# RWKV-7 recurrence of a streaming trunk: one elementwise step emitted later, one epilogue step earlier, filler matmuls moved

## The chip, the cores and the metric

One of the cores of a Trainium2 chip runs the whole program. The metric is device time in microseconds for one execution; lower is better. Every number below comes from the kernel before the change: its three timed runs, and one further execution that the hardware profiler recorded.

## The reference, cut to what matters

The program is one inference step of a small trunk over 1024 prompt rows and 8 x 16 sample rows (1152 in all), in float32. The part that the change touches is RWKV-7 time mixing; what is computed there:

```python
u = pr + (shifted - pr) * mu                       # token shift on the projected columns
r, k, v, wl, al, gl = split(u)
decay = exp(-exp(-softplus(-(w0 + tanh(wl) @ w2)) - 0.5))
a  = sigmoid(a0 + al @ a2);  g = sigmoid(gl) @ g2
kk = normalise(k * k_k);     k = k * (1 + (a - 1) * k_a)      # "key's part"
S_t = S_{t-1} * w_t + (S_{t-1} @ -kk_t) (kk_t a_t)^T + v_t k_t^T ;  y_t = S_t r_t
y  = groupnorm(y) * lnx_g + lnx_b
out = (y + sum(r * k * r_k) * v) * g
```

After it come forgetting attention, a gated merge and a SwiGLU block; these are not touched.

## The kernel before

The recurrence runs in chunks of 64 rows. Six units (`rwkv_unit`, called for unit 0 to 5) take 192 rows each: three chunks for all 8 heads, that is 12 blocks of two heads. Unit 5 is the last; it holds one prompt chunk and the sample rows, and has no next unit.

Inside a unit each chunk's delta rule becomes a triangular system. First the elementwise factors `BK` (L550 to L552) and `TT` (L559, L561) are made; then the Gram products (matmuls, masks L589); then a triangular inverse: VectorE inverts 16 x 16 diagonal blocks with thirty small operations (L623, L625) and turns the result twice (L637, L639); TensorE joins blocks in five steps: L661, copy `p0`; L669 and L672, followed by six VectorE additions into `x1c` and `x3`; L690, copied as `p1`; L699, copied into `x3`. Then the chunks follow one after the other: L736, L743, `w_sb`, L726, a copy into `SV4`, L748, `st`, L759, two additions, and the next chunk's L736.

TensorE's order is written out by hand: matmuls stand in its queue as the code emits them. Between the steps of the recurrence, `W(us)` emits filler: the k-steps ("pieces") of the input projection of later columns, `ceil(us / 0.52)` of them. One piece is three matmuls of 128x384 (L151, L152, L153: a float32 product in three parts), about 0.52 us by the constant `PIECE` in the code. The amount of filler over the whole program is fixed; what isn't placed here is run later. Outside of TensorE a scheduler sets each engine's order; operations inside `hi(...)` are preferred. Every queue then runs in order, and an instruction that waits holds up what stands behind it. ScalarE's queue also issues DMAs (stores of `g_s`, `oa_s`, `out_v_p`, `v_s`).

Two generators are stepped through from inside a unit:

- `prologue` of the next unit (`nxt`), seven steps: (1) `kr` L435 and its square L437; (2, 3) the two halves of the decay and iclr products L445, L446 with sigmoids L449, L450; (4) the norm's sums L454, logarithm L455, exponential L456; (5) the scan L463 and the exponentials L473 to L481; (6) **key's part**: L493 (x4), L494, L496, L500 (x4), all on VectorE; (7) the bonus L505, L506.
- `epilogue` of the unit before (`last`), three steps: (1) mean L514, L515, square L516, emitted behind the Gram products; (2) **variance**: matmuls L520, logarithm L521, exponential L522, then L523, L526, L527 on VectorE; (3) gate L532, L533 and the store `oa_s`.

Large tiles come from one ring, `tt_()`, of 13 slots: a new tile waits until all readers of the tile that had the slot are done. The small PSUM tiles come from rings too: `xs` for the products of the two generators (so L446 waits until a sigmoid, a logarithm or L533 has read an earlier one), `ms` for the rest.

Of the kernel before, what the change touches and what calls it, by code (L numbers as in the profile page):

```python
# [53 lines left out]
def hybrid_kernel(ctx: ExitStack, tc: tile.TileContext, d, o):  # L54
# [189 lines left out]
    def D(n):  # L244
        for _ in range(n):
            if fq:
                fq.pop(0)()
# [106 lines left out]
    def ms():  # L354
        return psr.tile([P, 512], F32, tag="ms", name="ms")
# [36 lines left out]
    def hi(f, *args, **kw):  # L392

        with tc.high_priority(offset=AHEAD):
            return f(*args, **kw)

    def W(us):

        D(int(math.ceil(us / PIECE)))
# [136 lines left out]
    def rwkv_unit(u_, us, nu, pre, last):  # L536
# [6 lines left out]
        nxt_pre, nxt, nus = {}, [], None  # L543

        def step(g):
            for x in g:
                next(x, None)
# [6 lines left out]
        def both(hd, i):  # L554
            return BK[HS[hd], i, 1 - hd:3 - hd, :].rearrange("p x t -> p (x t)")
# [25 lines left out]
        def masked(dst, src, c0, hs):  # L581
            n0 = 0
            late_ = [final and (c0 + n) % NC3 >= 1 for n in range(4)]
            while n0 < 4:
                n1 = n0 + 1
                while n1 < 4 and late_[n1] == late_[n0]:
                    n1 += 1
                mk = (gmask_s if late_[n0] else gmask)[hs].unsqueeze(1).broadcast_to([hs.stop - hs.start, n1 - n0, 2, C])
                V.tensor_tensor(dst[:, n0:n1], src[hs, n0:n1], mk, op=mult)  # L589
                n0 = n1  # L590

        for c0 in range(0, NC12, 4):
            pg = [(psr.tile([P, 512], F32, tag=f"y{x}", name="gram", bufs=1) if c0 == 4 else ms())
                  .rearrange("p (c y t) -> p c y t", c=4, y=2) for x in range(2)]
            for c in range(4):
                for hd in range(2):
                    T.matmul(pg[hd][:, c], both(hd, c0 + c), TT[HS[hd], c0 + c, hd], start=True, stop=True)
            for hd in range(2):
                masked(GB[HS[hd], c0:c0 + 4], pg[hd], c0, HS[hd])
                masked(TT[OP[hd], c0:c0 + 4, hd], pg[hd], c0, OP[hd])  # L600
            W(2.1)
        step(last)
        gab, grb = GB[:, :, 0, :], GB[:, :, 1, :]

# [32 lines left out]
        V.transpose(X1[:, 0:32, :], X[:, 0:32, :].rearrange("p t j -> p j t"))  # L637
        XL = inv_tile()
        V.transpose(XL[:, 0:32, :], X[:, 0:32, :])  # L639
        step(nxt)  # L640
        W(1.5)
        step(last)
        W(1.5)
        step(nxt)
        W(1.5)
        step(nxt)
        W(1.5)
        step(last)
# [1 line left out]
        step(nxt)  # L650
        W(1.5)
        step(nxt)
        W(3.1)
        xd = XL[:, 0:32, 0:NC12].rearrange("p t c -> p c t")
        QS = [slice(32 * q, 32 * q + 32) for q in range(4)]
        NB32 = NC12 * 32
# [23 lines left out]
        for q, qs in enumerate(QS):  # L680
            t0 = 32 * (q % 2)
            hi(V.tensor_tensor, x3[qs, :, t0:t0 + 32], p4[qs], xd[qs], op=add)
            if q % 2:
                hi(GP.memset, x3[qs, :, 0:32], 0.0)
        step(nxt)
        W(2.6)
        ps = ms()
        for c in range(NC12):
# [3 lines left out]
        p1 = tt_()[:, 0:NC12 * 32]  # L692
        for h0 in (0, 64):
            hi(S.copy, p1[h0 + 32:h0 + 64, :], ps[h0 + 32:h0 + 64, :NC12 * 32])
        W(1.5)
        ps = ms()
        for c in range(NC12):
            for h0 in (0, 64):
# [271 lines left out]
    with tc.manual_schedule(engines={mybir.EngineType.PE}):  # L970
        us, pre = unit_load(0), {}
        for _ in prologue(0, us, pre):
            W(5.0)
        W(2.0)
        last = []
        for u_ in range(NUN):
            us, pre, ep = rwkv_unit(u_, us, u_ + 1 if u_ + 1 < NUN else None, pre, last)
            last = [ep]
        for _ in last[0]:
            W(4.0)  # L980
# [52 lines left out]
    def head_load(h):  # L1033
        hs = slice(h * 64, (h + 1) * 64)
        need(*((kind, h // 2, g) for kind in "qkv" for g in range(NG)))
        flush()
        ka = fx.tile([P, SEQ], F32R, tag="ka", name=f"ka{h}", bufs=2)
        qa = fx.tile([P, SEQ], F32R, tag="qa", name=f"qa{h}", bufs=2)
        kb = fx.tile([68, SEQ], F32R, tag="kb", name=f"kb{h}", bufs=2)
        qb = fx.tile([68, SEQ], F32R, tag="qb", name=f"qb{h}", bufs=2)  # L1040
        vv = fx.tile([P, 8, 2, 64], F32R, tag="vv", name=f"vv{h}", bufs=2)
        for dst, srcs in ((ka, (kh_s[hs, :], kh_s[hs, :])), (qa, (qh_s[hs, :], ql_s[hs, :])),
                          (kb, (kl_s[hs, :], ka_s[h])), (qb, (qh_s[hs, :], qa_s[h]))):
            for x, s_ in enumerate(srcs):
                dma(dst[64 * x:64 * x + s_.shape[0], :].bitcast(F32), s_)
        for x in range(2):
            dma(vv[:, :, x, :].bitcast(F32), v2_s[:, x, hs].rearrange("(i p) e -> p i e", p=P))
        return ka, kb, qa, qb, vv
# [139 lines left out]
    nxt = head_load(0)  # L1188
    for h in range(8):
        hd = nxt  # L1190
        for g in range(2):
            pts = [prompt_scores(4 * g + j, *hd[:4]) for j in range(4)]
            prompt_pv(h, g, pts, *hd[4:], ())
            if g == 0 and h < 7:
                with tc.issue_after(turns[-2].ins) if h else ExitStack():
                    nxt = head_load(h + 1)
# [450 lines left out]
    with tc.tile_pool(name="fd", bufs=1, reuse_waits="tile", side="left") as fd, \  # L1647
# [7 lines left out]
        def down_ops(f):  # L1655
            raw = fd.tile([P, DM], F32, tag="wraw", name="raw_d", bufs=2)
            dma(raw, d["w_down"][0, f * P:(f + 1) * P, :])
            ar = fd.tile([P, NT], F32, tag="araw", name="raw_act", bufs=2)
            dma(ar, a_s[f * P:(f + 1) * P, :])
            wh = fd.tile([P, DM], F32R, tag="wh", name="hi_d", bufs=nbw)  # L1660
            wl = fd.tile([P, DM], F32R, tag="wl", name="lo_d", bufs=nbw)
            ah = fd.tile([P, NT], F32R, tag="ah", name="ah", bufs=nbw)
            al = fd.tile([P, NT], F32R, tag="al", name="al", bufs=nbw)
            split((wh, wl), raw)
            split((ah, al), ar)
            return wh, wl, ah, al
# [63 lines left out]
        for x in range(len(groups)):  # L1730
            nxt = [down_ops(f) for f in groups[x + 1]] if x + 1 < len(groups) else None
# [33 lines left out]
```

## Time and profile before

| | us |
|---|---|
| median of 3 runs (lowest, highest) | 2108.36 (2106.34, 2108.38) |
| the profiled execution: its own time | 2110.43 |
| the profiled execution: span on the core | 2108.4 |
| TensorE busy | 1980.6 (94% of the span) |
| VectorE busy | 1276.6 (61%) |
| ScalarE busy | 808.4 (38%) |
| mean granted TensorE clock | 0.969 of full speed |

The six units of the recurrence stand between about 190 and 800 us of the span. TensorE is busy or nearly so everywhere else. The page's slices show where it isn't: a digit under 9 in the row PE, a digit under 9 in the row PEclk. The rows that carry the argument are in their own section below. In a timeline a row gives the start, the duration, the engine, the line, the operation and the tiles, and in brackets how long the engine sat idle before it and what it waited for.

### The profile page before, as it was taken

The page shows a single profiled execution, that of the slowest core. Times are in us where ns is not written, and L with a number is a line of the kernel's source. Part 1 is how long each engine was busy: PE and PEld are TensorE (multiplying, and loading weights), DVE is VectorE, ACT ScalarE, POOL GpSimd, SP SyncE. Part 2 cuts the span into 40 slices and gives each one's busy share as a digit, 9 for nine tenths or more (in the row PEclk, how much of TensorE's full clock was granted, in tenths as well). Part 3 has the DMA queues.
Part 4 walks back from the last instruction along what each step waited for, and adds up shares of the span by engine and source line. Part 5 has one row for each costly group of instructions (what it writes and reads, how often), then busy time and mean ns, then how long its engine had stood idle before and what let it go on. Part 6 is the DMA issues. An engine that isn't in the chain of part 4 may idle for free. (4 is left out here: it accounts for less than half of the span.)

```text
span 2108.4 us, 38216 instructions
## 1 busy us (share of the span) xinstructions
PE 1980.6 (94%) x15472; PEld 1796.7 (85%) x15472; DVE 1276.6 (61%) x2414; ACT 808.4 (38%) x1567; POOL 187.1 (9%) x298
## 2 busy tenths in 40 slices
PE   7999988998899989789989899999999999799998
PEld 6999877787788978578867898999999999688887
DVE  5222777666766745578846528966666666454445
ACT  5322434362534432467744335523322323221113
POOL 1001000000000000010034236000000000000004
PEclk9999999999999999799999999999999999899999
DMA  4333333222221223677558544222222321542212
GB/s 158 105 101 98 108 92 97 70 66 67 66 70 53 80 80 95 155 202 201 138 180 258 173 146 150 73 74 63 83 63 69 99 63 53 207 149 85 85 64 90
DMA packets 221540, 228.41 MB, mean 108 GB/s; under 512 B 41534, under 2 KB 195796, under 8 KB 221364
## 3 DMA queue, kind: packets, MB, share of 16 engines
q1 hardware_dynamic: 158916, 159.33, 25.8%
q10 hardware_dynamic: 61920, 64.54, 9.1%
q8 instruction: 122, 2.00, 0.4%
q0 software_dynamic: 528, 2.10, 0.3%
q14 instruction: 54, 0.44, 0.1%
HBM read 157.00 MB, written 68.98 MB: 107 GB/s over the span
## 5 line engine op out<-in xcount | busy, mean ns | idle before, releaser
L151 PE MATMUL gm<-hh,hi_c 128*128 128x384 f32 (+1 forms) x1032 | 373.5, 362 | 2.5 <-DVE lg L916 0.7
L152 PE MATMUL gm<-hl,hi_c 128*128 128x384 f32 (+1 forms) x1032 | 351.3, 340 | 1.0 <-DVE hl L135 1.0
L153 PE MATMUL gm<-hh,lo_c 128*128 128x384 f32 (+1 forms) x1032 | 350.9, 340 | 0.0
L151 PEld LDWEIGHTS gm<-hh,hi_c 128*128 128x128 f32 (+1 forms) x1032 | 195.2, 189 | 19.7 <-issue 3.3
L152 PEld LDWEIGHTS gm<-hl,hi_c 128*128 128x128 f32 (+1 forms) x1032 | 195.7, 190 | 5.8 <-DVE hl L135 1.2
L153 PEld LDWEIGHTS gm<-hh,lo_c 128*128 128x128 f32 (+1 forms) x1032 | 195.2, 189 | 2.1
L1676 PE MATMUL dn<-hi_d,ah 128*128 128x512 f32 x396 | 156.2, 394 | 12.8 <-ACT ah L1383 12.1
L1677 PE MATMUL dn<-lo_d,ah 128*128 128x512 f32 x396 | 155.3, 393 | 0.0
L1678 PE MATMUL dn<-hi_d,al 128*128 128x512 f32 x396 | 155.3, 393 | 0.0
L1680 DVE TENSOR_TENSOR x<-x,dn 128x512 f32<-128x512 f32 x108 | 73.9, 686 | 118.3 <-PE dn L1678 116.7
L1676 PEld LDWEIGHTS dn<-hi_d,ah 128*128 128x128 f32 x396 | 75.2, 190 | 30.2 <-ACT ah L1383 13.4
L146 DVE TENSOR_TENSOR lo_c<-raw_c,hi_c 128x1024 fp32r<-128x1024 f32 (+1 forms) x43 | 51.5, 1199 | 70.2 <-ACT hi_c L145 70.1
L1696 POOL TENSOR_TENSOR yo<-x,gF 128x512 f32<-128x512 f32 x17 | 21.9, 1289 | 761.7 <-DVE x L1680 752.0
L1678 PEld LDWEIGHTS dn<-hi_d,al 128*128 128x128 f32 x396 | 75.1, 190 | 16.4 <-DVE al L1384 0.9
L1677 PEld LDWEIGHTS dn<-lo_d,ah 128*128 128x128 f32 x396 | 75.3, 190 | 15.5
L1383 ACT CAST ah<-raw_act 128x1152 fp32r<-128x1152 f32 x22 | 25.5, 1161 | 161.5 <-PE dn L1677 141.0
L1481 PE MATMUL po<-hi_o,mh 128*128 128x256 f32 x288 | 82.4, 286 | 0.0
L1482 PE MATMUL po<-lo_o,mh 128*128 128x256 f32 x288 | 82.3, 286 | 0.0
L1483 PE MATMUL po<-hi_o,ml 128*128 128x256 f32 x288 | 82.0, 285 | 0.0
L145 ACT CAST hi_c<-raw_c 128x1024 fp32r<-128x1024 f32 (+1 forms) x43 | 44.3, 1030 | 86.9 <-PE gm L152 81.9
L1564 DVE TENSOR_TENSOR buf<-buf,m 128x256 f32<-128x256 f32 (+1 forms) x88 | 39.7, 452 | 45.7 <-PE m L1542 45.7
L265 DVE SCALAR_TENSOR_TENSOR su<-gm,omu,sh 128x384 f32<-128x384 f32 (+1 forms) x42 | 24.0, 571 | 64.2 <-ACT sh L261 40.1
(500 smaller groups left out, 5354.9 us busy)
## 6 DMA issues: line engine op xcount, KB each, us to landing
raw_c<-in_w_in SPq DMA_DIRECT2D x42, 512.0 KB
raw_act<-a_s SPq DMA_DIRECT2D x22, 576.0 KB
raw_w_gate<-in_w_gate SPq DMA_DIRECT2D x22, 512.0 KB
raw_w_up<-in_w_up SPq DMA_DIRECT2D x22, 512.0 KB
raw_d<-in_w_down SPq DMA_DIRECT2D x22, 512.0 KB
g_s<-sg ACTq DMA_DIRECT2D x48, 192.0 KB
raw_o<-in_w_out SPq DMA_DIRECT2D x16, 512.0 KB
u_s<-su ACTq DMA_DIRECT2D x42, 192.0 KB
```

The lines of the kernel that those rows point to most:

```text
L145: S.copy(hi[:, :, c0:c0 + M], raw)
L146: eng.tensor_tensor(lo[:, :, c0:c0 + M], raw, hi[:, :, c0:c0 + M].bitcast(F32), op=sub)
L151: T.matmul(ps, wh(k), xh(k), start=(k == 0), stop=False)
L152: T.matmul(ps, wh(k), xl(k), start=False, stop=False)
L153: r = T.matmul(ps, wl(k), xh(k), start=False, stop=(k == nk - 1))
L1481: T.matmul(ps[:, :Q], mh, hi, start=(k == 0), stop=False)
L1482: T.matmul(ps[:, :Q], mh, lo, start=False, stop=False)
L1483: T.matmul(ps[:, :Q], ml, hi, start=False, stop=(k == NK - 1))
L1676: T.matmul(ps, ah[:, ts_], wh[:, cs], start=(x == 0), stop=False)
L1677: T.matmul(ps, ah[:, ts_], wl[:, cs], start=False, stop=False)
L1678: T.matmul(ps, al[:, ts_], wh[:, cs], start=False, stop=(x == n - 1))
L1680: r = V.tensor_tensor(xs, xs, ps, op=add)
```

## The change

Three edits, all in `rwkv_unit`:

1. In the Gram loop `W(2.1)` becomes `W(1.5)`: five pieces become three behind each of three groups.
2. In the inverse's stretch the epilogue's variance is emitted first, ahead of the prologue's `kr`; the pieces between the steps go from 3, 3, 3, 3, 2, 3, 6 to 3, 5, 5, 3, 2, 3, 5 (23 to 26).
3. Key's part (the prologue's sixth step) is no longer emitted between `x1c`/`x3` and L690, but behind the copies of `p1`; the filler behind those copies goes from 3 pieces to 5.

Each unit thus emits one piece less (-6, +3, +2).

```diff
@@ Gram loop
-            W(2.1)
+            W(1.5)
@@ inverse's stretch
         V.transpose(XL[:, 0:32, :], X[:, 0:32, :])
-        step(nxt)
-        W(1.5)
         step(last)
         W(1.5)
         step(nxt)
-        W(1.5)
+        W(2.1)
+        step(nxt)
+        W(2.1)
         step(nxt)
         W(1.5)
         step(last)
...
         step(nxt)
         W(1.5)
         step(nxt)
-        W(3.1)
+        W(2.6)
@@ behind x1c and x3
-        step(nxt)
         W(2.6)
         ps = ms()
...
             hi(S.copy, p1[h0 + 32:h0 + 64, :], ps[h0 + 32:h0 + 64, :NC12 * 32])
-        W(1.5)
+        step(nxt)
+        W(2.1)
         ps = ms()
```

What that does to the engines' orders, at three places.

ScalarE in unit 1, around the copies of `p1` (`COPY t<-ms 32x384`) and into `x3` (`COPY t<-ms 32x12x32`); `sg` is the merge gate, `[waits X]` names the engine whose semaphore an instruction waits for. Before:

```order
L953 ACTIVATE sg<-gm 128x384 [waits DMAHW1_49,PE_49]
L63 DMA g_s<-sg 128x384 [waits Activation_49]
L395 COPY t<-ms 32x384 [waits DVE_49]
L395 COPY t<-ms 32x384
L395 COPY t<-ms 32x12x32 [waits PE_49]
L395 COPY t<-ms 32x12x32
L395 COPY t<-cp 64x4x64 [waits DVE_49]
```

Now:

```order
L395 COPY t<-ms 32x384 [waits PE_49]
L395 COPY t<-ms 32x384
L953 ACTIVATE sg<-gm 128x384 [waits PE_49]
L63 DMA g_s<-sg 128x384 [waits DMAHW4_49,Activation_49]
L395 COPY t<-ms 32x12x32 [waits DVE_49,PE_49]
L395 COPY t<-ms 32x12x32
L395 COPY t<-cp 64x4x64 [waits DVE_49]
```

The copy of `p1` waited for VectorE (its slot of the ring held the first tile of key's part, read last by L494); it now waits for TensorE alone (its product L690, L689 in the changed file).

VectorE in unit 1, from the six additions behind L672 (`t<-ms,inv`) to the chunk's second half. Before:

```order
L395 TENSOR_TENSOR t<-ms,inv 32x12x32 x4
L493 TENSOR_SCALAR t<-t,prm,oka 128x192 x4
L494 TENSOR_TENSOR u<-t,u 128x768
L496 TENSOR_TENSOR t<-t 128x768
L500 SCALAR_TENSOR_TENSOR t<-u,prm 128x192 x4
L550 SCALAR_TENSOR_TENSOR BK<-t 128x12x64
L551 TENSOR_TENSOR BK<-u,t 128x12x64
L395 COPY w_sb<-cp 128x256
L552 TENSOR_TENSOR BK<-u,t 64x12x64
L395 COPY t<-cp 64x4x64
L395 TENSOR_TENSOR st<-cp,sc 128x256
L395 TENSOR_TENSOR t<-st,sts 64x4x64 x2
```

Now:

```order
L484 TENSOR_TENSOR sc<-sc,dmn 128x4x2
L146 TENSOR_TENSOR lo_c_3783<-raw_c_3780,hi_c_3782 128x1024
L493 TENSOR_SCALAR t<-t,prm,oka 128x192 x4
L494 TENSOR_TENSOR u<-t,u 128x768
L496 TENSOR_TENSOR t<-t 128x768
L395 COPY w_sb<-cp 128x256
L500 SCALAR_TENSOR_TENSOR t<-u,prm 128x192 x4
L395 COPY t<-cp 64x4x64
L550 SCALAR_TENSOR_TENSOR BK<-t 128x12x64
L551 TENSOR_TENSOR BK<-u,t 128x12x64
L395 TENSOR_TENSOR st<-cp,sc 128x256
L552 TENSOR_TENSOR BK<-u,t 64x12x64
```

Key's part itself starts at the same place, behind the six additions (with L484 and one `lo_c`, the low part of a projection weight, now between them; that pair stood ahead of the additions). `w_sb` has moved ahead of L500, the copy into `SV4` ahead of L550 and `st` ahead of L552. The two additions behind `st` follow L552 in both orders.

VectorE in unit 0, where the stores of the value columns fall (`tg`, `vl`: L929, L939; ScalarE's queue issues the stores of both). One piece of the difference, around the two transposes of the inverse:

```order
 L637 STREAM_TRANSPOSE inv<-inv 128x1024
 L639 STREAM_TRANSPOSE inv<-inv 128x1024
+L929 COPY tg<-pt 128x384
+L939 TENSOR_TENSOR vl<-pt,vh 128x384
 L463 SCALAR_TENSOR_TENSOR t<-rmask,t 128x768
 L929 COPY tg<-pt 128x384
 L146 TENSOR_TENSOR lo_c_2671<-raw_c_2668,hi_c_2670 128x1024
 L468 TENSOR_TENSOR t<-t,cm 128x768
```

The first `tg` and `vl` of the value columns stood ahead of L637, among the small operations L623 and L625; now they stand behind L639.

## Rows read from the trace of the kernel before

**Rows 1.** The page: busy time, share of the span and instructions of each engine.

```profile
PE 1980.6 (94%) x15472; PEld 1796.7 (85%) x15472; DVE 1276.6 (61%) x2414; ACT 808.4 (38%) x1567; POOL 187.1 (9%) x298
```

**Rows 2.** TensorE's waits, 180 to 780: line, releaser, total us, times, longest.

```profile
PE ms L699 <- ACT t L395: 19.8, 10, 4.4
PE xs L446 <- ACT t L449: 4.6, 5, 1.6
PE xs L446 <- ACT t L521: 4.4, 1, 4.4
...
PE ms L669 <- ACT t L395: 1.4, 2, 1.2
PE xs L454 <- DVE t L533: 1.2, 2, 1.1
```

**Rows 3.** Timeline of TensorE in unit 1, from L699 on.

```profile
395.92 0.31 PE L699 MATMUL ms<-t 32*32 32x32 f32 x2 [3.38 <-ACT t L395]
396.42 1.49 PE L699 MATMUL ms<-t 32*32 32x32 f32 x46 [0.18 <-ACT t L395]
397.83 1.12 PE L736 MATMUL cp<-t,TT 128*64 128x64 f32 x16
398.74 1.07 PE L743 MATMUL yps<-TT,t 128*64 128x64 f32 x16
```

**Rows 4.** Timeline of ScalarE in unit 1: the copies of p1.

```profile
395.40 0.97 ACT L395 COPY t<-ms 32x384 f32<-32x384 f32 x2 [3.37 <-DVE u L494]
```

**Rows 5.** Timeline of VectorE in unit 1, the same stretch.

```profile
387.14 5.13 DVE L395 TENSOR_TENSOR t<-ms,inv 32x384 f32<-32x384 f32 x6 [2.07 <-PE ms L672]
392.30 2.07 DVE L493 TENSOR_SCALAR t<-t,prm,oka 128x192 f32<-128x192 f32 x4
394.40 0.96 DVE L494 TENSOR_TENSOR u<-t,u 128x768 f32<-128x768 f32 x1
395.28 0.95 DVE L496 TENSOR_TENSOR t<-t 128x768 f32<-128x768 f32 x1
396.15 1.40 DVE L500 SCALAR_TENSOR_TENSOR t<-u,prm 128x192 f32<-128x192 f32 x4
397.46 0.95 DVE L550 SCALAR_TENSOR_TENSOR BK<-t 128x768 f32<-128x768 f32 x1
...
399.32 0.42 DVE L395 COPY w_sb<-cp 128x256 f32<-128x256 f32 x1
...
404.37 0.87 DVE L395 TENSOR_TENSOR t<-st,sts 64x256 f32<-64x256 f32 x2
...
407.29 1.23 DVE L146 TENSOR_TENSOR lo_c<-raw_c,hi_c 128x1024 fp32r<-128x1024 f32 x1
```

**Rows 6.** Stretches, additions behind L672 to second L736, units 0 to 4: length, engines' busy, clock.

```profile
387.14:406.10 18.96, 15.40 (x219) 13.33 (x219) 15.85 (x26) 2.81 (x7) 1.14 (x2) 0.82 0.18 54
...
sum 97.35, PE 77.42 PEld 67.17 DVE 82.92 ACT 18.60 POOL 5.71; mean PE 15.48 PEld 13.43 DVE 16.58 ACT 3.72 POOL 1.14
```

**Rows 7.** One stretch of unit 1: length, busy times (PE, PEld, DVE, ACT, POOL), granted clock.

```profile
394.40:401.20 6.80, 5.10 (x87) 4.34 (x89) 6.26 (x10) 1.88 (x4) 0.00 (x0) 0.53 0.01 2
```

**Rows 8.** Timeline of TensorE in unit 5, which has no key's part.

```profile
740.40 0.95 PE L699 MATMUL ms<-t 32*32 32x32 f32 x48
741.27 0.69 PE L736 MATMUL cp<-t,TT 128*64 128x64 f32 x16
741.79 0.64 PE L743 MATMUL yps<-TT,t 128*64 128x64 f32 x16
```

**Rows 9.** Timeline of VectorE in unit 2: the inverse's transposes to the gate.

```profile
452.86 2.04 DVE L637 STREAM_TRANSPOSE inv<-inv 128x1024 f32<-128x1024 f32 x1
454.84 1.19 DVE L639 STREAM_TRANSPOSE inv<-inv 128x1024 f32<-128x1024 f32 x1
...
460.74 0.53 DVE L533 TENSOR_TENSOR t<-t,xs 128x384 f32<-128x384 f32 x1
```

**Rows 10.** Timeline of ScalarE in unit 1: the variance's logarithm behind a store of vl.

```profile
361.78 1.28 ACT L521 ACT_TABLE_LOAD   x1 [2.08 <-DVE vl L939]
```

## The prediction

> **What bounds the kernel now.** I read the busy times first, then TensorE's waits, then the timelines of the three engines behind the longest wait. TensorE is busy 94% of the span [rows 1], so the time is its work plus its idle time plus what a halved clock costs; the work is the same before and after, because filler that isn't placed here is run later. The change can therefore only move idle time and clock. The list of TensorE's waits [rows 2] gives, in the stretch of the recurrence, 19.8 us before L699 and 11.6 us in four groups of the inverse's stretch (L446 twice, L669, L454).
>
> The 19.8 us are one thing five times. In unit 1 TensorE sits 3.38 us before L699 [rows 3], since ScalarE copies `p1` only at 395.40; ScalarE had been idle 3.37 us, until VectorE's L494 ended [rows 4]. VectorE was then in the middle of the six additions (5.16 us, 387.14 to 392.30) and key's part: L493 2.10, L494 0.88 [rows 5]. `p1` doesn't read any of that; it takes the ring slot of L493's tile. Behind the wait the granted clock is 0.53 over 6.8 us [rows 7], so nearly all of that time at the lower level, 1.2 instead of 2.4 GHz. There L699 takes 0.31 + 1.49, L736 1.12 and L743 1.07 [rows 3]; in unit 5, without key's part, the wait or the clock's fall, 0.95, 0.69 and 0.64 [rows 8]. The halved clock costs 0.85 + 0.43 + 0.43 = 1.7 us a unit. Unit 5 gains nothing here.
>
> **Key's part behind the copies: the price by VectorE.** The wait can't simply vanish, since VectorE is busy 15.85 of the 18.96 us from the additions' start to the second chunk's L736 in unit 1, and 82.92 of 97.35 us over the five units [rows 6]. Key's part still stands behind the additions, and the chunk's copies now stand between its pieces. I walk VectorE's new order for unit 1 with start-to-start times [rows 5]: additions 5.16; L484 and `lo_c` 1.3 (1.23 for `lo_c`, overlapped by 0.1, and an estimated 0.17 for the 8-element L484); L493 2.10; L494 0.88; L496 0.87; `w_sb` 0.45; L500 1.31; copy into `SV4` 0.45; L550 and L551 0.87 each; `st` 0.46; L552 0.88; the two additions 0.90. Sum 16.5 us, and L736 of the second chunk waits for its end. TensorE's own work in that stretch is 15.40 busy [rows 6] - 1.7 for the clock + 2 x 0.52 for the two pieces that L699's filler gains = 14.7 us. VectorE is longer, so it becomes the bound: 16.5 us, with some 1.8 us of idle TensorE left, split between L726 (for `w_sb`), L748 (for the copy) and L736 (for the additions).
>
> The gain in unit 1 is 18.96 - 16.5 + 1.04 (pieces done there that were run later) = 3.5 us. For units 0, 2, 3, 4 the same walk with what stands in their orders (no L484 behind the additions in 2 to 4: 16.35; two small low parts more in unit 0: 17.0, an estimate) makes 82.55 us in all against 97.35 [rows 6]: 14.8 + 5 x 1.04 = **20.0 us**. Bounds: if VectorE's work slipped wholly beside TensorE's, 5 x 1.8 = 9 us more; if each hand-over between the engines costs 0.3 us more than I count (four in a unit), 6 us less. I take the walk, because its terms are rows of the same stretch. If the idle left over still halves the clock, TensorE's 14.7 become 16.4, still no more than VectorE's 16.5: the cost is 0 to 1.7 us a unit, near the lower end, 0.3.
>
> **Variance first and the moved filler: the inverse's stretch.** Old waits that should go: L446 behind the sigmoids, 4.6 us, since five pieces instead of three stand between its halves and the variance's two table loads are over earlier; L669's 1.4, since `p0`'s copy now stands ahead of the exponential L456 on ScalarE; L454's 1.2. The single 4.4 us (unit 1, L446 behind L521) is ScalarE's queue held by a store of `vl`: L521's table load waits 2.08 us for L939 [rows 10]. Together 11.6 us [rows 2].
>
> New waits. (a) Six Gram pieces less and, from the mean's matmul to L454, four more: TensorE reaches L454 about 1.0 us sooner, and up to 1.6 us more where L446's wait is gone (4.6 us over five times, the longest 1.6 [rows 2]). L454 needs the slot that L533 reads. It waits for that only 1.2 us in all units together now [rows 2], but there is nothing to spare: both come at about the same time. VectorE's chain there (both transposes 3.2 us, normalisation, scan) doesn't shorten. So a new wait of 2.0 us in units 2 to 4: 6 us; bounds 0 (the chain moves up wholly with the Gram products) and 2.5 each. (b) Unit 0: `vl` now stands behind both transposes, 2.04 + 1.19 us later [rows 9]; ScalarE's in-order queue holds its store, and behind it the second half's sigmoids, then L454's logarithm and `p0`. I take 6.4 us, two waits of that length, bounds one and two. (c) Unit 1: the same kind of block sits before L532 instead of L446: 4.4 us [rows 2], and 0.9 more before L632, an estimate; bounds 0 and 5.3. Sum 17.7, less 11.6: a **loss of 6.1 us**, from -11.6 to +7.6.
>
> The Gram loop itself I cost at nothing: no Gram product is in the list of waits, and what hides the removed pieces' time is the rest of the filler; if all six pieces became waits it would be 3.1 us a unit. Three more table loads on ScalarE (1.28 us each [rows 10]) lie beside its idle time; on the path they would be 3.8 us.
>
> **Sum.** 20.0 - 6.1 = 13.9 us off the profiled execution's 2110.43 (span 2108.4 and 2.0 around it): 2096.5. The median of the runs, 2108.36, lies 2.07 below that execution: 2094.5, rounded to **2094 us**.
>
> **Rivals.** *A: the inverse's stretch takes most of it back.* ScalarE's queue blocked by `vl` in units 0 and 1 twice each, and L454 waiting 2.5 us in all others: losses up to 25 us against 11.6, and the key stretches at their lower bound of 14: 2108.36 - 14 + 13 = 2107. For it: the waits are of kinds that the trace has. Against: value columns fall in two units only.
>
> *B: slower.* L454 waits for L533 in all five units. From the first transpose to L533's end VectorE takes 8.4 us (452.86 to 460.74 + 0.53 [rows 9]); if TensorE reaches L454 as that chain starts, 5 x 8.4 = 42 us against 20.0 + 11.6: 2119. It decides from 7.2 us a unit on (31.6 us, and 4.2 for a difference that shows). Against: TensorE gets ahead by only 1.0 to 2.5 us.
>
> *C: better.* VectorE's chain follows the Gram products up, so (a) is nothing and (b) is one block of 3.2: losses 8.5 instead of 17.7, gain 23: 2085. If in addition VectorE's walk hides beside TensorE, 9 us more: 2076.
>
> The Trainium skill, "TensorE: Matmul & The Clock Gate", in the sections "Terms" and "What's actually happening", tells that the throttled level is the default, that activity releases it, and that the penalty is the throttled time times the share of pulses held back. By that, unit 1's 6.8 us would have cost 3.4 us, not the 1.7 that its longer instructions show: much of the stretch is waiting, which a clock doesn't lengthen. With it TensorE's stretch would be 13.0 instead of 14.7 and case C's last figure 2067 instead of 2076; the forecast, bound by VectorE, stays.
>
> That the change doesn't do what it says I exclude: in the new order the copy of `p1` waits for TensorE alone.
>
> **How the numbers follow.** About 0.2% (4.2 us) is what a measurement of this kernel can tell from no change. Forecast, 2088 to 2100: 0.52. C, below 2088: 0.20. A, 2100 to 2112: 0.22. B: 0.06. Range for 8 in 10: half of C's cases lie above 2083, and most of A's below 2107: 2083 to 2107. Faster (below 2104.1): forecast, C and a quarter of A: 0.78. Same: 0.15. Slower: B and a little of A: 0.07.
>
> **What would show it.** Right: no wait of L699 on ScalarE over 0.5 us; the five stretches from the additions to the second L736 at 16.3 to 17.0 us; small waits at L726, L748 and L736 on VectorE instead; granted clock there near full. For the loss: waits of L454 on L533 near 2 us in units 2 to 4, L446 gone, unit 0 with a wait behind `vl`'s store. Wrong: L699 still waiting; stretches of 18 us, which would mean that hand-overs cost more than counted; waits over 4 us at L454 or L532 in more than one unit.

## The result and the profile after

The changed kernel takes 2084.65 us (median of 3, 2082.52 to 2084.72) against 2108.36: ratio 0.9885, 95% interval 0.9869 to 0.9900, 23.7 us faster. The forecast was 2094, the range 2083 to 2107: the direction and the range hold, the gain was put 40% too low.

The page of the changed kernel, engines' busy time (answers to [rows 1]):

```profile
PE 1969.0 (95%) x15472; PEld 1790.2 (86%) x15472; DVE 1268.3 (61%) x2414; ACT 811.5 (39%) x1570; POOL 188.6 (9%) x298
```

The span is 2082.9 us. Both kernels execute the same 15472 matmuls, so a difference in TensorE's busy time is put down to its clock. That is argued from equal work, and the traces bear it out: over the fourteen profiled executions of this document busy time rises by 0.8 us for each us of clock pulses held back, (1 - clock) x span (a straight line through them, an estimate; correlation 0.97). It splits the 25.5 us between the two profiled executions: idle time 2108.4 - 1980.6 = 127.8 before and 113.9 after, **13.9 us**; busy time 1980.6 - 1969.0 = **11.6 us**, with a mean granted clock of 0.969 before and 0.975 after. The Trainium skill, "TensorE: Matmul & The Clock Gate", section "Terms", prices throttled time at the share of pulses held back. By that, (1 - 0.969) x 2108.4 - (1 - 0.975) x 2082.9 = 13.3 us, an estimate; the trace shows 11.6 and so nearly agrees over the whole program, where unit 1's stretch alone had shown half of that price.

TensorE's waits of the changed kernel in the same window as [rows 2] (line, releaser, total, times, longest):

```profile
PE cp L726 <- DVE w_sb L395: 6.6, 6, 1.9
PE gm L151 <- DVE vl L939: 4.1, 1, 4.1
PE ms L632 <- ACT t L634: 3.2, 3, 1.5
...
PE cp L748 <- ACT t L395: 2.4, 3, 0.8
...
PE ms L689 <- DVE t L395: 1.0, 1, 1.0
PE xs L454 <- DVE t L533: 0.9, 1, 0.9
PE ms L669 <- ACT t L395: 0.6, 1, 0.6
```

L699 and L446 are gone from the list. L726 and L689 are new and L748 has grown from 0.3 us to 2.4; 8.0 of their 10.0 us stand in the five stretches that key's part held up. (L804's 2.6 us, in the sample rows of unit 5, are new too.) The stretches from the end of L672 to the second chunk's L736 (L736 of unit 1 at 395.09), columns as in [rows 6]:

```profile
286.12:304.34 18.22, 14.44 (x228) 12.63 (x225) 16.32 (x28) 4.21 (x9) 1.15 (x2) 1.00 0.31 98
379.74:395.09 15.35, 14.25 (x227) 12.57 (x225) 14.96 (x26) 4.80 (x11) 1.15 (x2) 1.00 0.25 74
...
543.11:561.83 18.72, 17.20 (x227) 15.25 (x224) 16.75 (x28) 5.42 (x11) 1.15 (x2) 0.82 0.21 63
...
sum 82.81, PE 74.44 PEld 65.62 DVE 77.93 ACT 22.57 POOL 5.74; mean PE 14.89 PEld 13.12 DVE 15.59 ACT 4.51 POOL 1.15
```

Five stretches are 82.8 us long; before, [rows 6] gave 97.35 (97.8 from the end of L672). In units 1, 2 and 4 the granted clock is 1.00 and the length 15.3; unit 3 has clock 0.82 and 18.7, unit 0 starts its additions 2.1 us late. VectorE in unit 1 (answers to [rows 5]):

```profile
379.85 5.14 DVE L395 TENSOR_TENSOR t<-ms,inv 32x384 f32<-32x384 f32 x6 [1.85 <-PE ms L672]
385.02 0.17 DVE L484 TENSOR_TENSOR sc<-sc,dmn 128x8 f32<-128x8 f32 x1
385.11 1.22 DVE L146 TENSOR_TENSOR lo_c<-raw_c,hi_c 128x1024 fp32r<-128x1024 f32 x1
386.24 1.24 DVE L493 TENSOR_SCALAR t<-t,prm,oka 128x192 f32<-128x192 f32 x4
387.52 0.96 DVE L494 TENSOR_TENSOR u<-t,u 128x768 f32<-128x768 f32 x1
...
389.37 0.42 DVE L395 COPY w_sb<-cp 128x256 f32<-128x256 f32 x1
...
394.52 0.87 DVE L395 TENSOR_TENSOR t<-st,sts 64x256 f32<-64x256 f32 x2
```

VectorE runs without a gap from 379.85 on, as the walk had it, and L736 follows the first half of the last two additions. One term is smaller: four L493 take 1.24 us, not the 2.07 of [rows 5]; the eighth experiment below shows why.

### The profile page after: what moved, and what is told of

Its sections match the earlier page's. It is cut to its first block, busy times and chain, and to the rows that moved or that the text cites. A ratio compares the mean times of both kernels' runs of the same rounds, so it can differ in the third digit from the quotient of the medians.

```text
span 2082.9 us, 38230 instructions
## 1 busy us (share of the span) xinstructions
PE 1969.0 (95%) x15472; PEld 1790.2 (86%) x15472; DVE 1268.3 (61%) x2414; ACT 811.5 (39%) x1570; POOL 188.6 (9%) x298
## 5 line engine op out<-in xcount | busy, mean ns | idle before, releaser
L151 PE MATMUL gm<-hh,hi_c 128*128 128x384 f32 (+1 forms) x1032 | 371.5, 360 | 5.1 <-DVE vl L939 4.1
L151 PEld LDWEIGHTS gm<-hh,hi_c 128*128 128x128 f32 (+1 forms) x1032 | 194.1, 188 | 20.9 <-issue 7.0
L1383 ACT CAST ah<-raw_act 128x1152 fp32r<-128x1152 f32 x22 | 25.5, 1160 | 161.5 <-PE dn L1677 141.8
## 6 DMA issues: line engine op xcount, KB each, us to landing
raw_c<-in_w_in SPq DMA_DIRECT2D x42, 512.0 KB
raw_w_gate<-in_w_gate SPq DMA_DIRECT2D x22, 512.0 KB
raw_w_up<-in_w_up SPq DMA_DIRECT2D x22, 512.0 KB
raw_d<-in_w_down SPq DMA_DIRECT2D x22, 512.0 KB
raw_o<-in_w_out SPq DMA_DIRECT2D x16, 512.0 KB
```

The lines of the kernel that those rows point to most:

```text
L151: T.matmul(ps, wh(k), xh(k), start=(k == 0), stop=False)
```

## The experiments

All times are medians; ratios are against the kernel before on the same chip. Idle is the span less TensorE's busy time. Span, busy, idle and clock are those of one profiled execution each; the kernel before, run 25 times beside the experiments, took 2106.0 to 2113.6 us at clocks of 0.966 to 0.973, so a few us of busy time say little about an edit. Edit 1 is the Gram loop's filler, 2 the inverse's stretch, 3 key's part behind the copies.

| kernel | us | ratio (95%) | span | busy | idle | clock |
|---|---|---|---|---|---|---|
| before | 2108.4 to 2110.5 | | 2108.4 | 1980.6 | 127.8 | 0.969 |
| changed (1, 2, 3) | 2084.65 | 0.9885 (0.9869 to 0.9900) | 2082.9 | 1969.0 | 113.9 | 0.975 |
| e1: 3 | 2099.33 | 0.9955 (0.9940 to 0.9970) | 2097.2 | 1982.2 | 115.0 | 0.969 |
| e2: 1, 2 | 2094.03 | 0.9930 (0.9911 to 0.9949) | 2089.6 | 1964.1 | 125.5 | 0.976 |
| e3: `p1` without a slot | 2096.82 | 0.9935 (0.9918 to 0.9952) | 2089.3 | 1970.8 | 118.5 | 0.974 |
| e4: 2, 3 | 2087.71 | 0.9898 (0.9881 to 0.9914) | 2085.6 | 1973.6 | 112.0 | 0.973 |
| e5: 1, 3, order of 2 | 2083.33 | 0.9870 (0.9843 to 0.9898) | 2080.6 | 1967.3 | 113.3 | 0.976 |
| e6: 1, 3, amounts of 2 | 2084.62 | 0.9877 (0.9851 to 0.9903) | 2086.1 | 1970.0 | 116.1 | 0.974 |
| e7: changed, v stores on SyncE | 2080.80 | 0.9863 (0.9844 to 0.9881) | 2080.7 | 1968.1 | 112.6 | 0.977 |
| e8: e3 with a later clearing | 2088.67 | 0.9901 (0.9882 to 0.9919) | 2089.0 | 1973.0 | 116.0 | 0.973 |
| e9: 1 | 2120.77 | 1.0055 (1.0039 to 1.0070) | 2117.8 | 1988.2 | 129.6 | 0.965 |
| e10: 1, 3 | 2078.09 | 0.9856 (0.9843 to 0.9868) | 2076.6 | 1963.7 | 112.9 | 0.980 |
| e11: changed, e7's and e8's edits | 2079.36 | 0.9865 (0.9852 to 0.9877) | 2077.5 | 1966.9 | 110.6 | 0.978 |
| e12: e11, old amounts of 2 | 2080.86 | 0.9875 (0.9858 to 0.9891) | 2079.7 | 1963.1 | 116.6 | 0.978 |

**e1, key's part alone.**

```diff
-        step(nxt)
         W(2.6)
...
-        W(1.5)
+        step(nxt)
+        W(2.1)
```

> Key's part behind the copies of p1 (and 5 instead of 3 pieces there) alone; Gram loop and inverse's stretch as before. Theory now (the move is worth what VectorE's walk gave, 15 to 20 us, and the other two edits are worth some 5 us more): L699's wait gone, 2089 to 2093 us, with the 14 us of waits of the inverse's stretch (L446, L632, L669, L454) still there. Rival, the prediction's term (the other two edits lose 6 us): faster than the full change, about 2079 us.

2099.3 us, 9.3 less: the prediction's rival is out, and the theory's 15 to 20 is missed too. TensorE's waits of this kernel:

```profile
PE cp L726 <- DVE w_sb L395: 8.3, 5, 1.9
PE xs L446 <- ACT t L449: 7.6, 5, 2.8
...
PE xs L446 <- ACT t L521: 2.6, 1, 2.6
```

L699's wait is gone and 8.3 us at L726 have come. Idle time falls by 12.8 us, but TensorE's busy time is 1.6 us longer than before: over the whole program the move by itself gives the idle time, and no clock. Where the clock was won and lost again is worked out in the next section.

**e2, the other two edits alone.** (The changed kernel without the lines above.)

> Fewer Gram pieces and variance first alone; key's part stays ahead of L690. Theory now: the waits before L699 stay (18 to 20 us over five units), those of the inverse's stretch fall from 14 to 9 us or less, 2102 to 2106 us. Rival, the prediction's term: new waits of L454 of 2 us in units 2 to 4 and a longer block in unit 0, 2112 to 2115 us.

```profile
PE ms L699 <- ACT t L395: 20.3, 10, 4.4
PE pt L927 <- ACT sg L906: 6.5, 1, 6.5
PE xs L454 <- DVE t L533: 2.9, 3, 1.2
```

2094.0 us, below the theory's band and far from the prediction's 2112 to 2115. L446 is gone, but a wait of 6.5 us stands at L927 in its place, L454's have grown from 1.2 to 2.9, and L699's 20.3 us are all there. Idle falls by only 2.3 us; the gain is TensorE's busy time, 16.5 us less. So edits 1 and 2 do almost nothing for waiting in this pairing. By place (next section) the recurrence is 14.2 us shorter, 9.9 of it for 19 pieces that left it, and the hand-over to attention, which took them, is shorter too.

**e3, the slot.** `p1` is put into the free half of `p0`'s tile; nothing moves.

```diff
-        p0 = tt_()[:, 0:NB32]
+        p01 = tt_()
+        p0 = p01[:, 0:NB32]
...
-        p1 = tt_()[:, 0:NC12 * 32]
+        p1 = p01[:, NB32:2 * NB32]
```

> The kernel before with one edit: p1 is put into the unused half of p0's tile, so that it needs no slot of the ring; nothing is moved. Theory: the slot alone made L699 wait, so its wait goes (under 1 us a unit) and 13 to 18 us with it, 2090 to 2095 us. Rival (where key's part stands on VectorE is what matters, not the slot): the copies come earlier but the chunk then waits as long as before at L726 and L736, 2105 to 2109 us.

```profile
PE cp L727 <- DVE w_sb L395: 9.2, 6, 1.9
```

2096.8 us, 1.8 past the theory's band and far from the rival's. L699's 19.8 us (L700 here) shrink to 0.4, and 9.2 us appear at `w_sb` (L727 here), 1.7 to 1.9 a unit: the wait was the ring slot's, and VectorE is the next bound, as the prediction had it. Time and interval overlap with e1's: for L699, moving key's part and freeing the slot are the same cure.

**e4, the Gram filler back to five pieces in the changed kernel.**

```diff
-            W(1.5)
+            W(2.1)
```

> The changed kernel with the Gram loop's filler back at 5 pieces each (six pieces more a unit there). Theory now (VectorE's chain starts from the Gram products, so filler between them moves TensorE and the chain alike and costs or gives no wait): 2083 to 2088 us, waits at L454 as in the changed kernel (0.9 us) within 1 us. Rival, the prediction's step (fewer Gram pieces bring TensorE to L454 too early): the wait at L454 goes and the time falls by 1 to 3 us, 2081 to 2083.

```profile
PE xs L446 <- ACT t L449: 2.5, 1, 2.5
PE xs L454 <- ACT t L449: 1.9, 1, 1.9
...
PE xs L454 <- DVE t L533: 0.3, 1, 0.3
```

2087.7 us, within the theory's band; the wait of L454 on L533 is 0.3 instead of 0.9, while two waits behind the sigmoids L449 appear (2.5 at L446, 1.9 at L454). So the Gram filler moves L454's wait by 0.6 us, not by the 6 us that the prediction put on it. Idle is 1.9 us less than in the changed kernel, busy 4.6 more, and executions of one kernel differ by more than that in time (7.6 us before the change).

**e5 and e6, edit 2 taken apart.** e5 has the new order with the old amounts, e6 the old order with the new amounts.

```diff
-        W(2.1)
+        W(1.5)
         step(nxt)
-        W(2.1)
+        W(1.5)
...
-        W(2.6)
+        W(3.1)
```

```diff
-        step(last)
+        step(nxt)
         W(1.5)
-        step(nxt)
+        step(last)
         W(2.1)
```

> The changed kernel with the old amounts of filler in the inverse's stretch (3, 3, 3, 3, 2, 3, 6 pieces), variance still first. Theory A (it is the two more pieces ahead of each half of L446's products that hide ScalarE's sigmoids): waits of L446 behind L449 come back, 1 to 2 us a unit, 2089 to 2094 us. Theory B (the order alone, variance ahead of the prologue, does it): no such waits, 2083 to 2087 us.

> The changed kernel with the prologue's kr emitted first again and variance second, the new amounts of filler kept (3, 5, 5, 3, 2, 3, 5). Theory A (the amounts do it): within 3 us of the changed kernel, 2083 to 2088 us, waits of L446 under 2 us in all. Theory B (the order does it, since variance's two table loads and its place in ScalarE's queue then stand right ahead of the sigmoids): waits of L446 of 5 to 10 us in all, 2091 to 2097 us.

TensorE's waits of e5 and then of e6:

```profile
PE xs L446 <- ACT t L449: 6.1, 4, 2.6
PE ms L669 <- ACT t L395: 2.9, 1, 2.9
```

```profile
PE xs L454 <- DVE t L533: 3.7, 3, 1.6
...
PE xs L532 <- ACT t L449: 1.6, 1, 1.6
```

On the waits theory A is right: L446's come back with the old amounts (6.1 us) and stay away with the new ones. On the time e5 misses theory A's 2089 to 2094: both runs are level with the changed kernel (2083.3 and 2084.6), so neither half of edit 2 is worth anything measurable on top of 1 and 3.

**e7, the stores of the value columns from SyncE's queue.**

```diff
-                        dma2(v2_s[:, x, ct * P:(ct + 1) * P]
+                        dma(v2_s[:, x, ct * P:(ct + 1) * P]
```

> The changed kernel with the stores of vh and vl (v_s) issued from SyncE's queue instead of ScalarE's. Theory (ScalarE's queue is held by the store that waits for vl, which costs 4.1 us in unit 1 and 1 to 2 us in unit 0): these waits go, 2079 to 2082 us. Rival (SyncE's queue then holds its loads behind the stores, or TensorE waits for vl itself and not for ScalarE): 2084 us or more.

```profile
PE gm L151 <- DVE vl L939: 1.8, 1, 1.8
PE xs L532 <- ACT t L449: 1.8, 1, 1.8
```

2080.8 us, in the theory's band, though the intervals overlap and the runs were not made side by side. The wait on `vl` goes from 4.1 to 1.8, and 1.8 come back at L532: idle falls by 1.3 us only. Both waits stand in unit 1, 3.6 us together, so the store in ScalarE's queue accounts for 0.5 of the 4.1 us there; the rest is the part of the rival that has TensorE wait for `vl` itself.

**e8, the clearing.** In e3's kernel GpSimd's clearing of the next unit's inverse tile is made to wait for L494.

```diff
+        GP.tensor_copy(X[:, 0, 0:1], k2[:, 0:1])
         GP.memset(X, 0.0)
```

> The kernel of e3_half_tile with GpSimd's clearing of the next unit's inverse tile (L616, 0.98 us) made to wait until key's L494 is done (a one-column copy from it ahead of the clearing). Theory (the first L493 is held while GpSimd clears: 1.2 us against 0.36 for the others): the four L493 take 1.24 instead of 2.07 us in units 0 to 4, and 2 to 4 us of VectorE-bound time go, 2092 to 2095 us. Rival (the first L493 is slow for another reason): 2.07 stays, 2095 to 2098 us.

In e3, VectorE's L493 and GpSimd's clearing in unit 1:

```profile
390.15 2.07 DVE L493 TENSOR_SCALAR t<-t,prm,oka 128x192 f32<-128x192 f32 x4
```

```profile
390.27 0.98 POOL L616 MEMSET inv<- 128x1056 f32 x1 [10.21 <-DVE t L395]
```

In e8, and then the spread of all 24 L493 there (shortest, median, longest ns):

```profile
388.53 1.25 DVE L493 TENSOR_SCALAR t<-t,prm,oka 128x192 f32<-128x192 f32 x4
```

```profile
391.74 0.98 POOL L617 MEMSET inv<- 128x1056 f32 x1
```

```profile
L493 DVE TENSOR_SCALAR t<-t,prm,oka x24: 372/375/382, 212.5 to 640.7; 128x192 f32<-128x192 f32 x24
```

With the clearing out of the way the four take 1.25 us; the longest single one falls from 1208 ns (in the changed kernel) to 382. TensorE's wait at `w_sb` falls from 9.2 to 5.3 us:

```profile
PE cp L728 <- DVE w_sb L395: 5.3, 6, 1.1
```

The cause of the slow L493 is settled. What it is worth in time is not: the 2088.7 us lie below the theory's band, the medians of e3 and e8 are 8.1 us apart with intervals that just touch, the two profiled executions (2089.3 and 2089.0) are level, with 2.5 us less idle time and 2.2 more busy time.

**e9, the Gram filler alone, and e10, edits 1 and 3.** By then the suspicion was that filler put off to the start of attention is free there, because TensorE idles there anyway.

> The kernel before with the Gram loop's filler alone cut from 5 to 3 pieces (36 pieces less in the recurrence; they run later, in the hand-over to attention). Theory H (filler that is put off costs less than its 0.52 us there, because TensorE idles in the hand-over anyway): all waits of the recurrence stay within 2 us of before, L699's too, and the time falls by 5 to 12 us, 2097 to 2104 us. Rival (a piece costs the same wherever it runs): 2106 to 2111 us.

> Edits 1 and 3 without edit 2: key's part behind the copies of p1, fewer Gram pieces, the inverse's stretch in its old order and with its old amounts. Theory H: edit 1 gives its share here too, 2085 to 2092 us, with waits of L446 of about 10 us in all still there. Rival (edit 2 is needed, since it alone removes the waits of L446): 2095 to 2100 us, no better than edit 3 alone.

```profile
PE ms L699 <- ACT t L395: 19.0, 10, 4.4
PE xs L446 <- ACT t L449: 7.1, 4, 2.7
```

```profile
PE xs L446 <- ACT t L449: 8.0, 4, 3.4
PE cp L726 <- DVE w_sb L395: 7.8, 5, 2.3
```

e9 is 11.6 us **slower** (1.0055, clear of 1), past the bands of theory and rival alike. Its idle time is 1.8 us more than before and its busy time 7.6 us more, at the lowest clock in the table, 0.965. The same edit on top of e1 gives 2078.1, below theory H's band, 21 us less than e1 and the best of all kernels here, with 8.0 us of L446's waits still in it; its idle time is 2.1 us under e1's, its busy time 18.5 us under e1's. One edit costs 11.6 us or gives 21, and in both cases most of the difference is busy time, which is put down to the clock. e10's interval ends just below the changed kernel's: on top of 1 and 3, edit 2 gave nothing and may have cost some 6 us.

**e11 and e12, all that helped, put together.** e11 is the changed kernel with e7's and e8's lines; e12 takes the old amounts of edit 2 back as well.

> The changed kernel with the stores of vh and vl issued from SyncE and GpSimd's clearing made to wait for L494. Theory: 4 us by the stores and 1 to 2 us by the clearing (in units 0 and 3 alone it still meets L493), 2077 to 2081 us. Rival (the two don't add up, since VectorE isn't the bound where the stores waited): 2080 to 2084 us.

> The kernel of e11_full_plus with the old amounts of filler in the inverse's stretch (three pieces less a unit, run later). Theory H: the pieces put off cost next to nothing in the hand-over, the waits of L446 that come back cost 4 to 6 us; within 3 us of e11_full_plus. Rival (put-off filler costs its full time): 3 to 6 us slower than e11_full_plus.

2079.4 and 2080.9 us, the first in its theory's band, the second within 3 us of the first as theory H had it. e11 has the least idle time of all, 110.6 us, and its time is level with e10's, whose clock is higher; its interval overlaps the changed kernel's, so what e7's and e8's lines add is not shown. e12 has 6.0 us more idle and 3.8 us less busy time.

## Why the prediction was right or wrong

*L699's wait is the ring slot of key's first tile.* Right: the list of waits has lost it, and e3 takes it away by the slot alone.

*VectorE becomes the bound, 82.55 us for five stretches, 20.0 us gained.* Right in sum: from the end of L672, 97.8 - 82.8 + 5.2 for the pieces = 20.2. Two terms inside were off and cancelled. Units 1, 2 and 4 are some 1.2 us shorter than walked, since L493 no longer meets GpSimd's clearing (2.07 - 1.24 = 0.8) and L736 starts after half of the additions (0.3). Units 0 and 3 are longer than walked: unit 0's additions wait 2.1 us for a low part that itself waits for a store, and unit 3 has the clock at the lower level for two spells.

*The halved clock costs little there.* Wrong where it came: unit 3, with two spells of it, takes 18.72 us where units 2 and 4 take 15.3, so 3.5 us, and not the 0 to 1.7 of the text. The 1.7 us were too few from the start, since they counted L699, L736 and L743 alone and the pieces and L726 stand in the same spell; unit 1's TensorE, busy 15.51 us from the end of L672 before, is busy 14.25 now with 1.04 us of pieces more, which makes 2.3. In unit 3 the clock falls without a listed wait ahead of it: between 492 and 555 none is listed, and what stands ahead is the run of small 32x32 products L661, L669, L672. Granted clock in the changed kernel around it (columns as in [rows 7]):

```profile
541.00:544.00 3.00, 3.00 (x114) 2.96 (x104) 0.96 (x1) 2.97 (x5) 0.82 (x2) 0.90 0.02 6
544.00:547.00 3.00, 3.00 (x11) 3.00 (x10) 2.55 (x4) 0.86 (x3) 0.00 (x0) 0.53 0.32 119
...
557.00:560.00 3.00, 3.00 (x36) 2.32 (x35) 2.63 (x4) 0.15 (x1) 0.00 (x0) 0.51 0.65 175
```

*The inverse's stretch loses 6.1 us.* **This is the step that failed.** The listed waits at L632, L151, L454 and L669 are 8.8 us after the change; before, they were 14.0 (the 11.6 of [rows 2], 1.8 at L632, 0.6 at L151). So it gained 5.2 us where a loss of 6.1 was put: 11.3 us of the 11.6 by which the profiled gain (25.5) exceeds the forecast one (13.9). By the text's own bounds its best case was a gain of 8.4, not of 11.6, since (b) was never put under one wait of 3.2. Term (a), 6 us, was 0.9: the Gram pieces that go bring TensorE and VectorE forward alike, because VectorE's chain starts from the Gram products, the bound of 0 that the text named; e4 bears it out, with 0.3 when the pieces are back. Counted from L632's first product in unit 2, TensorE came to L454 18.66 us later before (442.66 to 461.32) and 18.6 after:

```profile
442.66 0.59 PE L632 MATMUL ms<-ident,BK 64*128 64x64 f32 x12
...
461.32 1.13 PE L454 MATMUL xs<-t,ones_b 128*128 128x384 f32 x3
```

```profile
429.44 0.59 PE L632 MATMUL ms<-ident,BK 64*128 64x64 f32 x12
...
448.05 0.81 PE L454 MATMUL xs<-t,ones_b 128*128 128x384 f32 x2
449.74 0.91 PE L454 MATMUL xs<-t,ones_b 128*128 128x384 f32 x2 [0.88 <-DVE t L533]
```

Four pieces more stand there instead of L446's wait; the 0.88 us that L454 now waits come from one `lo_c` that has moved ahead of L533 on VectorE. Term (b), 6.4 us in unit 0, was 0.6 at L669 and 1.0 at L689, with 1.8 at L632 and no L446 (L689's 1.0 lies in the five stretches and is counted there): what stands behind `vl`'s store came nearly in time. Term (c) had the size right and the place wrong: unit 1's block is 4.1 us, at L151, where TensorE waits for `vl` itself and not for ScalarE.

*Work is constant, so only idle time and clock move.* Right as a frame: idle time behaves roughly as a sum of edits (1: +1.8; 3: -12.8; 1 and 2: -2.3; all: -13.9; 1 and 3: -14.9; 2 and 3: -15.8; sums miss by up to 4 us), busy time doesn't (1: +7.6; 3: +1.6; 1 and 2: -16.5; all: -11.6; 1 and 3: -16.9; 2 and 3: -7.0; sums miss by up to 26 us). The forecast priced the clock in the five stretches only, 8.5 us. There it came. Sums of the five stretches from the end of L672, as above, of the kernel before, of e1 and of e2:

```profile
sum 97.82, PE 77.89 PEld 67.64 DVE 82.94 ACT 18.71 POOL 5.71; mean PE 15.58 PEld 13.53 DVE 16.59 ACT 3.74 POOL 1.14
sum 85.89, PE 76.66 PEld 67.26 DVE 79.34 ACT 19.39 POOL 5.74; mean PE 15.33 PEld 13.45 DVE 15.87 ACT 3.88 POOL 1.15
sum 98.82, PE 77.38 PEld 67.05 DVE 83.83 ACT 19.72 POOL 5.71; mean PE 15.48 PEld 13.41 DVE 16.77 ACT 3.94 POOL 1.14
```

With 5.2 us for the pieces that edit 3 adds, TensorE is busy 8.7 us less in the changed kernel (74.44) and 6.4 less in e1, and 0.5 less in e2, which keeps L699's wait. So in these stretches the clock followed that wait: granted 0.82 to 0.84 in all five before, 0.76 to 0.91 in e2, 1.00 in four of five in the changed kernel. e1 lost the 6.4 us and 1.6 more elsewhere. That the whole program's 11.6 came near 8.5 is luck, as e1 shows, where the same term came and the total did not.

By place, from the same traces: the recurrence from 190 us to the end of unit 5's L672, the hand-over from there to the attention's first L1323, and the rest; in brackets TensorE's matmuls (a piece is three of them).

| kernel | recurrence us | hand-over us | rest us |
|---|---|---|---|
| before | 545.0 (5607) | 351.0 (2111) | 1022.4 |
| changed | 514.3 (5581) | 356.3 (2134) | 1022.3 |
| e1: 3 | 536.9 (5631) | 342.6 (2083) | 1027.7 |
| e2: 1, 2 | 530.8 (5550) | 343.5 (2165) | 1025.3 |
| e4: 2, 3 | 529.0 (5691) | 347.3 (2025) | 1019.3 |
| e9: 1 | 535.4 (5500) | 366.9 (2221) | 1025.5 |
| e10: 1, 3 | 512.0 (5531) | 350.7 (2188) | 1023.9 |

The changed kernel's gain stands in the recurrence. The hand-over's length doesn't follow the pieces that it gets: in all kernels here but e9 it takes 343 to 361 us, in no order, for 2025 to 2189 matmuls, though 164 more are 55 pieces, 28 us at 0.52. So the premise that a piece put off costs its 0.52 us later is not borne out there; e10's 26 pieces cost nothing, and e2's 18 came with a hand-over 7.5 us shorter. Only e9, with 37 more, takes 15.9 us longer, and its recurrence is 9.6 us shorter although 36 pieces, 18.5 us, have left it. Each row is one execution, and why the hand-over and the clock outside of the five stretches come out as they do stays open.

Rival C came nearest (2085), and for the reason that it gave. A, B and the case that nothing changes are out.

## What to carry to other kernels

Split a measured difference into idle and busy time of the engine that bounds the kernel, and by place, before giving it to an edit: here the busy part, put down to the clock, didn't add up over edits, and part of it stood far from the lines that were edited. A copy that waits for an engine it has no data from may be waiting for a tile's slot, as here; look for a half-used tile before moving code. When filler is taken from ahead of a chain, ask whether the chain's start moves with it, and compare arrivals from a common event, not from the clock on the wall.

## What the runs showed of the hardware

A write-only clearing on GpSimd (0.98 us) holds a VectorE `tensor_scalar` of 128x192 float32 until it is over: the first of the four L493 takes 1207 ns instead of 370, in each of units 0 to 4 of the kernel before. By the recorded starts L493 began 0.1 us ahead of the clearing (392.30 against 392.41 in unit 1) and was held all the same. `lo_c`, a tensor_tensor, ran beside the same clearing at its usual 1.22 us (385.11 in the list of VectorE above). The Trainium skill, "SBUF — State Buffer", section "Who interferes with whom", says that `tensor_scalar` in its two-port form and GpSimd exclude each other for a whole instruction, and that a tensor_tensor contends only with a GpSimd instruction that reads; e8 and these rows agree.
